# A two-layer hybrid backbone on one core: where the conditioning products are issued, and how their weights lie in memory

## The chip, the cores and the metric

One core of one Trainium2 chip. The metric is the device time of one execution in microseconds; before the change the median of three runs is 2308.41 us (2298.91 to 2311.32).

## What is computed

Two layers of a diffusion backbone on 512 latent and 256 context tokens (768 in all) with 1024 features, in fp32. Each layer mixes tokens in three groups of heads that share one input projection and one output projection: latent attention with 8 heads, a gated DeltaNet (GDN, a scan over chunks of 64 tokens), and a gated linear attention (GLA, in two directions). A gated feed-forward with a convolution over tokens follows. Every sub-layer is wrapped in norms and in scale, shift and gate, which come from two conditioning vectors, one for latents and one for context:

```python
mod_x = [m[:, None, :] for m in jnp.split(jax.nn.silu(c) @ w_ada[i] + b_ada[i], N_MOD, axis=-1)]
mod_c = jnp.split(jax.nn.silu(c_ctx) @ w_ada[i] + b_ada[i], N_MOD, axis=-1)
hx = modulate(rmsnorm(x, norm_mix_pre[i]), mod_x[0], mod_x[1])
y_c, y_x = token_mixing(...)
x = x + mod_x[2] * rmsnorm(y_x, norm_mix_post[i])
hx = modulate(rmsnorm(x, norm_ffn_pre[i]), mod_x[3], mod_x[4])
x = x + mod_x[5] * rmsnorm(conv_ffn(hx, ...))
```

`w_ada` is 1024 x 6144 for each layer, 24 MB. Its six products are needed at different times: 0 and 1 ahead of the input projection, 2 behind the output projection, 3 and 4 ahead of the feed-forward, 5 behind it.

## The kernel before, in words

An fp32 product is made of three passes over operands split in two float32r parts. `wsplit` (L197) loads 512 KB of weights into a tile `wr` of a ring of three (`raw`, L194), and ScalarE (`wh`, L191) and VectorE (`wl`, L192) split it; `fprod` (L217) issues the products into the large PSUM banks `bb`. Small products take the banks a, b, c and d; `ab` (L183) gives them out in turn, among those that the phase names.

A layer runs as follows (`layer`, L311). `project_in` (L555) makes 20 blocks of the input projection; the GDN's preparation and scan are chains of small products, and `pace` feeds steps of the large products between them. `mla_project` makes keys, queries and values and stores them in DRAM (`Kd`, `Qd`). Then comes `attention` for pair 0 of the heads, `gla`, and `attention` for pairs 1 to 3. `pair` (L1303) loads the keys and queries of a pair into tiles of the ring `wr`, three or four loads for each pair. Then follow the products of `w_out`, a norm, and the feed-forward with 40 blocks of `ffn_w_in` and the products back. Pair 0 draws small banks from a and d, pairs 1 to 3 from a and b; GLA's own products take c and d.

GLA makes the products inside its chunks by halving: seven levels for the context and seven for the latents, each on VectorE (L1180 to L1183), ScalarE, GpSimd, VectorE and GpSimd (L1193), TensorE (banks c and d) and VectorE again (the predicated copies of L1202). Then it makes two and four output tiles (L1229).

The framework orders the instructions of each engine ahead of time, by priorities and a simulated timeline; each engine then executes its own list in order. Tiles of a ring are given out in program order: a load waits until the third tile before it has been read.

The conditioning products are a generator, `ada` (L466). An item of it is one of six modulations and a quarter of 1024 columns: two loads of 512 KB of `w_ada` (L478) into ring tiles, eight products with the vectors as stationary operand (16 records `a<-wr,cTs` in the trace, in one of the banks), a copy by ScalarE (`part`, L485), two products that add up the parts and transpose them (four records `a<-cst,part`), and a copy by VectorE into `modT` (L488). `tick(n)` (L458) runs n items of the generators in `self.bg`. Eight items of layer 0 (modulations 0 and 1) lead the program, with tiles of their own (`aw`). The other 16 of layer 0 (`later`) are put in `self.bg` in `project_in`, behind the first blocks of the GDN, and each further block ticks one. The 24 of layer 1 are put there at the start of layer 0's feed-forward, whose blocks tick one each:

```python
        if LM == 2:
            self.bg += later          # in project_in
...
        if not last:
            self.bg.append(self.ada(l + 1, range(6)))   # ahead of the feed-forward
```

Of the kernel before, what the change touches and what calls it, by code (L numbers as in the profile page):

```python
# [17 lines left out]
PSUM = bass.MemoryType.PSUM  # L18
# [3 lines left out]
T = 768  # L22
# [10 lines left out]
# columns of the feature-major parameter array  # L33
# [16 lines left out]
LM = 2  # L50
# [8 lines left out]
NF = 3                  # tiles of the GDN preparation under way at a time  # L59
# columns of the constant array  # L60
# [50 lines left out]
def rope_tables():  # L111
    """cos and signed sin on the rope rows, ones on the others: even heads, odd heads"""
# [23 lines left out]
class Net:  # L136
# [46 lines left out]
    def ab(self, tags=None):  # L183
        """a bank of PSUM, out of those of the phase or of the chain of work named"""
        tags = tags or self.tags
        self.turn[tags] = n = self.turn.get(tags, -1) + 1
        t = tags[n % len(tags)]
        return self.ps.tile([128, 512], F32, name=self.nm(t), tag=t, bufs=1)
# [8 lines left out]
    def wsplit(self, src, n=1024):  # L197
        """loads [128, n] weights and splits them in two float32r parts, 512 columns a piece"""
# [18 lines left out]
    def fprod(self, ps, wh, wl, xh, xl, segs, nk, order=None, off=256):  # L217
        """ps[:, 256 + token] = sum over k of w[:, k]^T x[k], in three float32r passes"""
# [13 lines left out]
    def pace(self, n):  # L232
        """some steps of the products that fill the tensor engine beside chains of small ones"""
# [7 lines left out]
    def rsqrt(self, out, ss, scale, bias):  # L241
        """out = 1 / sqrt(scale * ss + bias), small tiles"""
# [18 lines left out]
    def main(self):  # L261
# [20 lines left out]
        # the first two modulations lead; the norm needs all of x, then them  # L282
# [28 lines left out]
    def layer(self, l, later):  # L311
# [9 lines left out]
        # token mixing  # L321
# [11 lines left out]
        self.project_in(later)  # L333
# [10 lines left out]
        # pairs that need nothing of what the scan holds up run beside its end  # L344
# [17 lines left out]
        self.attention(A2, range(EP[l], 4), mh, ml, mixed)  # L362
        self.xt = []
# [9 lines left out]
        # output projection, norm, residual  # L373
# [17 lines left out]
        # feed-forward  # L391
        self.ph = 2
        self.tags = "abcd"
        if not last:
            self.bg.append(self.ada(l + 1, range(6)))
# [6 lines left out]
        def tail(s):  # L402
            """norm, residual, and the next layer's first norm for a segment"""
# [33 lines left out]
    def coefs(self, s, r):  # L437
        """modulation of sub-layer s for latent (0) or context (1) tokens: scale [128, 8], shift [128, 8]"""
# [8 lines left out]
    def gate(self, s):  # L447
        """gate times post-norm gain of sub-layer s: [128, 8] for latent and context tokens"""
# [17 lines left out]
    def ada(self, l, mods, raw=None):  # L466
        """products of the conditioning vectors with w_ada, a load at a time"""
# [3 lines left out]
        for m in mods:  # L471
            for h in range(4):
                c0 = m * 1024 + h * 256
                raws = []
                for k in range(2):
                    rt = (raw or self.raw)()
                    src = self.a["w_ada"][l, k * 512:(k + 1) * 512, c0:c0 + 256].rearrange("(k p) c -> p k c", p=128)
                    nc.sync.dma_start(rt.rearrange("p (k c) -> p k c", k=4), src)  # L478
# [13 lines left out]
    def rms(self, N, src, a, b, copy=False):  # L492
        """1 / rms over the features of tokens a..b, on all partitions (in PSUM)"""
# [32 lines left out]
    def post(self, N, s, seg, y, g=None):  # L526
        """x += gate * norm(y)"""
# [8 lines left out]
    def prenorm(self, N, s, seg, rb=None):  # L536
        """norm and modulation of x, in two float32r parts"""
# [17 lines left out]
    def project_in(self, later):  # L555
# [12 lines left out]
        def gate(x):  # L568
            """silu times the head norm's gain, kept in DRAM"""
# [10 lines left out]
        def misc():  # L580
            # rope key, GLA low rank, GDN gates
# [12 lines left out]
            # GLA's gates by direction: softplus of the negated, kept in DRAM  # L594
# [16 lines left out]
        # GDN: k, v, q; token-major, sums of squares of k and q  # L611
        Gp, self.G = self.pool("G", "right")
        self.ktok, self.vtok, qtok = tok(self.F, "ktok"), tok(self.F, "vtok"), tok(self.G, "qtok")
        ss = self.small(48, "kss")              # [k | q, t, h]
# [24 lines left out]
        def projections():  # L639
            # GLA: k, q, v token-major, kept in DRAM  # L640
# [50 lines left out]
        if LM == 0:  # L691
            self.bg += later
# [857 lines left out]
```

## Time and profile before

| | before |
|---|---|
| runs, us | 2298.91, 2308.41, 2311.32 (median 2308.41) |
| profiled execution: first to last instruction, us | 2300.4 |
| mean granted clock of TensorE | 0.935 |
| TensorE matmul busy, us | 2073.8 (90%) |
| VectorE busy, us | 1308.2 (57%) |
| ScalarE busy, us | 1008.7 (44%) |
| GpSimd busy, us | 536.1 (23%) |
| DMA, MB | 235.64 |
| 512 KB loads of w_ada into the ring | 80 |

The profiled execution's time is its span, 8 us under the median of the three runs and close to the fastest. PE is TensorE's matmuls, PEld its weight loads, DVE VectorE, ACT ScalarE, POOL GpSimd, SP the engine that issues DMAs. Busy shares are means over stages with different limits, so the rows further down are from single stages. In layer 0 of this execution the conditioning items of `project_in` lie between 100 and 375 us, the GDN scan between 266 and 478, GLA with attention beside it from 482 to 655, the products of `w_out` from there, and the feed-forward's conditioning items between 763 and 988.

### The profile page before, as it was taken

Reading aid. Unit: us, or ns where it says so; the run is one execution under the profiler, and the core shown is the slowest. Engines: PE = TensorE matmul, PEld = TensorE weight load, DVE = VectorE, ACT = ScalarE, POOL = GpSimd, SP = SyncE. Lnnn points to the kernel's source line nnn. Section 1 sums busy time; section 2 is a strip of 40 time slices with the busy share of each in tenths; the row PEclk is TensorE's granted clock in tenths of the full one; section 3 lists DMA queues with packets and bytes.
Section 4 is the critical chain, followed back from the end, with each engine's and each line's share of the span. In section 5 each row is a group of like instructions: output and inputs, shape, how many; then the busy total and the mean of one; then the engine's idle time right before and its main releaser. Section 6 shows DMA issues by size and latency. Waiting matters only on the chain. (4 is left out here: it accounts for less than half of the span.)

```text
span 2300.4 us, 44608 instructions
## 1 busy us (share of the span) xinstructions
PE 2073.8 (90%) x18168; PEld 1695.2 (74%) x18168; DVE 1308.2 (57%) x2474; ACT 1008.7 (44%) x1927; POOL 536.1 (23%) x897
## 2 busy tenths in 40 slices
PE   6898999988988799999999889899978887999996
PEld 3676877766667578888888677777766666888886
DVE  3454435678736743445454774555657647655566
ACT  4653323566454533323232456434446346543333
POOL 1442122245402310101010334322123503211102
PEclk9899999999899899999999987999988888999997
DMA  7233344421042454421222332122402043332322
GB/s 259 73 111 104 102 152 151 148 79 58 8 158 92 142 169 165 163 85 56 65 66 72 111 98 76 42 73 93 149 26 95 6 166 95 111 98 95 101 92 92
DMA packets 121998, 235.64 MB, mean 102 GB/s; under 512 B 9088, under 2 KB 74048, under 8 KB 121792
## 3 DMA queue, kind: packets, MB, share of 16 engines
q1 hardware_dynamic: 121792, 232.78, 30.9%
q8 instruction: 143, 2.34, 0.4%
q14 instruction: 63, 0.52, 0.1%
HBM read 204.04 MB, written 28.70 MB: 101 GB/s over the span
## 5 line engine op out<-in xcount | busy, mean ns | idle before, releaser
L212 PE MATMUL bb<-hh,wl 128*128 128x512 f32 (+1 forms) x1520 | 549.3, 362 | 17.6 <-DVE wl L192 8.0
L212 PE MATMUL bb<-hl,wh 128*128 128x512 f32 (+1 forms) x1520 | 545.0, 359 | 7.3 <-POOL hl L552 5.5
L192 DVE TENSOR_TENSOR wl<-wr,wh 128x512 fp32r<-128x512 f32 (+2 forms) x452 | 336.2, 747 | 364.8 <-ACT wh L191 363.7
L212 PE MATMUL bb<-hh,wh 128*128 128x512 f32 (+1 forms) x1520 | 541.2, 356 | 0.0
L191 ACT CAST wh<-wr 128x512 fp32r<-128x512 f32 (+2 forms) x452 | 274.4, 612 | 527.4 <-PE bb L212 359.2
L212 PEld LDWEIGHTS bb<-hh,wl 128*128 128x128 f32 x1520 | 294.2, 194 | 74.2 <-issue 11.1
L212 PEld LDWEIGHTS bb<-hl,wh 128*128 128x128 f32 x1520 | 294.2, 194 | 53.0 <-POOL hl L552 9.8
L212 PEld LDWEIGHTS bb<-hh,wh 128*128 128x128 f32 x1520 | 294.4, 194 | 39.9 <-issue 2.4
L212 PE MATMUL bb<-g,wh 128*128 128x512 f32 (+1 forms) x1024 | 264.0, 349 | 2.3 <-DVE g L192 2.3
L1426 POOL TENSOR_SCALAR y<-u,fmt 128x512 f32<-128x512 f32 (+2 forms) x88 | 81.3, 925 | 524.1 <-ACT u L811 522.6
L212 PEld LDWEIGHTS bb<-g,wh 128*128 128x128 f32 x1024 | 181.9, 195 | 27.6 <-DVE g L192 3.3
L212 PE MATMUL bb<-g,wl 128*128 128x512 f32 (+1 forms) x512 | 180.6, 354 | 21.5 <-DVE wl L192 8.5
L212 PEld LDWEIGHTS bb<-g,wl 128*128 128x128 f32 x512 | 99.4, 195 | 36.9 <-ACT g L191 9.3
L212 PE MATMUL bb<-mh,wl 128*128 128x256 f32 (+1 forms) x256 | 84.8, 332 | 22.5 <-DVE wl L192 15.4
L811 ACT ACTIVATE u<-bb,fmt 128x512 f32<-128x512 f32 (+1 forms) x118 | 69.1, 614 | 81.1 <-PE bb L212 81.0
L1453 DVE TENSOR_TENSOR y<-y,bb 128x512 f32<-128x512 f32 (+2 forms) x80 | 54.7, 685 | 82.9 <-PE bb L212 82.8
L507 POOL TENSOR_TENSOR acc<-acc,sq 128x256 f32<-128x256 f32 (+1 forms) x48 | 49.4, 1031 | 185.2 <-ACT sq L505 184.5
L1427 DVE SCALAR_TENSOR_TENSOR y<-u,fmt,y 128x512 f32<-128x512 f32 (+2 forms) x88 | 72.3, 822 | 28.9 <-POOL y L1426 28.9
L1365 ACT ACTIVATE P<-bb,ast,srq 128x768 f32<-128x768 f32 (+1 forms) x80 | 72.5, 907 | 30.5 <-DVE ast L1363 20.2
L212 PE MATMUL bb<-ml,wh 128*128 128x256 f32 (+1 forms) x256 | 83.5, 326 | 0.5
L212 PE MATMUL bb<-mh,wh 128*128 128x256 f32 (+1 forms) x256 | 82.2, 321 | 0.0
L1362 DVE TENSOR_REDUCE ast<-bb 128x1 f32<-128x768 f32 (+1 forms) x80 | 67.3, 844 | 25.3 <-PE bb L212 25.0
(509 smaller groups left out, 3720.1 us busy)
## 6 DMA issues: line engine op xcount, KB each, us to landing
wr<-in_ffn_w_in SPq DMA_DIRECT2D x92, 512.0 KB, 3.5
wr<-in_w_ada SPq DMA_DIRECT2D x80, 512.0 KB, 4.4
wr<-in_ffn_w_out SPq DMA_DIRECT2D x48, 512.0 KB, 3.5
wr<-in_w_in SPq DMA_DIRECT2D x40, 512.0 KB, 4.0
wr<-in_w_out SPq DMA_DIRECT2D x32, 512.0 KB, 3.5
aw<-in_w_ada SPq DMA_DIRECT2D x16, 512.0 KB, 8.9
x<-in_xT SPq DMA_DIRECT2D x16, 384.0 KB, 8.5
wr<-in_w_uq SPq DMA_DIRECT2D x16, 192.0 KB, 2.6
```

Source lines behind the costliest of these rows:

```text
L191: self.nc.scalar.copy(hi, src)
L192: (eng or self.nc.vector).tensor_tensor(lo, src, hi.bitcast(F32), op=ALU.subtract)
L212: self.nc.tensor.matmul(out, l, r, start=start, stop=stop)
L507: (nc.vector, nc.gpsimd)[k % 2].tensor_tensor(acc[k % 2], acc[k % 2], sq, op=ALU.add)
L811: nc.scalar.activation(u[:, a + o:b + o], ps[:, off + a:off + b], AF.Identity, bias=bias)
L1362: nc.vector.reduce_max(st[:, 0:1], sc, axis=AX)
L1365: nc.scalar.activation(P[:, :w], sc, AF.Exp, bias=st[:, 0:1], scale=self.srq[:, t:t + 1], accum_out=st[:, 1:2])
L1426: nc.gpsimd.tensor_scalar(yv, u[:, lo + 1:lo + 1 + n], cw[1], self.fm(P_FCB + i), op0=ALU.mult, op1=ALU.add)
L1427: nc.vector.scalar_tensor_tensor(yv, u[:, lo:lo + n], cw[0], yv, op0=ALU.mult, op1=ALU.add)
L1453: nc.vector.tensor_tensor(y, y, p, op=ALU.add)
```

## The change

Items move. The 16 items `later` of layer 0 and the 24 of layer 1 are put in `self.bg` ahead of attention of pair 0 in layer 0. Attention ticks one item for each query tile (six for each pair), GLA one for each level and one for each output tile; what is left after attention is drained. `project_in` and layer 0's feed-forward have none to tick any more. On the host `w_ada` is packed anew, so that a load of 512 KB has rows of 4 KB on 128 partitions instead of 1 KB rows, four for each partition; the products read the same bytes. Comments are dropped, and lines move by up to four.

```diff
@@ layer
-        self.project_in(later)
+        self.project_in()
...
         A2p, A2 = self.pool("A2")
+        self.bg += later
+        if not last:
+            self.bg.append(self.ada(l + 1, range(6)))
         with self.ahead(HA):
             self.attention(A2, range(EP[l]))
...
         self.attention(A2, range(EP[l], 4), mh, ml, mixed)
+        self.tick(99)
...
         self.tags = "abcd"
-        if not last:
-            self.bg.append(self.ada(l + 1, range(6)))
         Up, U = self.pool("U", "right")
@@ ada
-                c0 = m * 1024 + h * 256
...
-                    src = self.a["w_ada"][l, k * 512:(k + 1) * 512, c0:c0 + 256].rearrange("(k p) c -> p k c", p=128)
-                    nc.sync.dma_start(rt.rearrange("p (k c) -> p k c", k=4), src)
+                    nc.sync.dma_start(rt, self.a["w_ada"][l, 4 * m + h, k])
@@ project_in
-        if LM == 0:
-            self.bg += later
         drain(gdn(0))
-        if LM == 2:
-            self.bg += later
@@ gla, at the end of a level and of an output tile
+                self.tick(1)
...
+                self.tick(1)
@@ attention, at the end of a query tile
+                self.tick(1)
@@ pack
-    out["w_ada"] = f["w_ada"]
+    out["w_ada"] = f["w_ada"].reshape(L, 2, 4, 128, 24, 256).transpose(0, 4, 1, 3, 2, 5).reshape(L, 24, 2, 128, 1024)
```

The order of each engine's instructions moves with it, at two places above all. The first is SyncE's queue of loads, behind the weights of the values (`in_w_uv`). Before, it holds the loads of pair 1's keys and queries, then pair 2's, ahead of GLA's (`gv`, `h`):

```order
L200 DMA wr_5078<-in_w_uv 128x1024
L1314 DMA wr_6362<-Kd_688_4766 128x768
...
L1314 DMA wr_6368<-krope_437 128x768
...
L1314 DMA wr_6378<-Qd_713_4872 128x768
...
L1314 DMA wr_6384<-Qd_738_4990 128x768
L1314 DMA wr_6763<-Kd_694_4789 128x768
...
L1078 DMA gv_5517<-gvd_2272 128x1536
L1092 DMA h_5523<-gkd_2270 128x256
```

Now the loads of 25 conditioning items come first, of which the first and the last stand here; pair 1's follow them, the last one behind GLA's last store (`md`):

```order
L199 DMA wr_4790<-in_w_uv 128x1024
L478 DMA wr_4929<-in_w_ada 128x1024
...
L478 DMA wr_4931<-in_w_ada 128x1024
...
L478 DMA wr_6469<-in_w_ada 128x1024
...
L478 DMA wr_6471<-in_w_ada 128x1024
L1312 DMA wr_6525<-Kd_624_4478 128x768
L1312 DMA wr_6531<-krope_437 128x768
L1312 DMA wr_6541<-Qd_649_4584 128x768
L1046 DMA md_112_436<-zt_6380 256x1x256
L1312 DMA wr_6547<-Qd_674_4702 128x768
```

All of these loads but GLA's use the ring `wr`. Pair 1's four loads moved from right behind `in_w_uv` to behind the 50 loads of the 25 items.

The second is TensorE's order inside GLA. Before, products of a context level (`c<-q,x`, `d<-q,x`) stand between query-key products of pair 1 (`bb<-K,Q`), its transposes (`a<-cst,P`) and its products with the values (`b<-PT,V`):

```order
L212 MATMUL bb_6671<-K_1039_6364,Q10l_6381 128x256
L212 MATMUL bb_6671<-K_1040_6365,Q10h_6380 128x256
L212 MATMUL bb_6671<-K_1039_6364,Q10h_6380 128x256
L212 MATMUL c_5632<-q_901_5629,x_5622 64x128 x4
L212 MATMUL d_5638<-q_901_5629,x_5622 64x128 x4
L212 MATMUL b_6513<-PT_6502,V_5131 64x128
...
L215 MATMUL a_6547<-cst,P_6541 128x128 x4
...
L212 MATMUL c_5654<-q_905_5651,x_5644 64x128 x4
L212 MATMUL d_5660<-q_905_5651,x_5644 64x128 x4
```

Now only conditioning items (`a<-wr,cTs`, `a<-cst,part`) stand between the levels' products:

```order
L211 MATMUL a_5628<-wr_5624,cTs 32x256 x4
L211 MATMUL d_5588<-wr_5584,cTs 32x256 x4
L211 MATMUL d_5588<-wr_5586,cTs 32x256 x4
L211 MATMUL c_5612<-q_893_5609,x_5602 64x128 x4
L211 MATMUL a_5628<-wr_5626,cTs 32x256 x4
L211 MATMUL d_5588<-cst,part_5597 128x2 x2
L211 MATMUL c_5652<-q_901_5649,x_5642 64x128 x4
L211 MATMUL d_5618<-q_893_5609,x_5602 64x128 x4
L211 MATMUL a_5628<-cst,part_5637 128x2 x2
L211 MATMUL c_5684<-q_858_5437,x_5682 64x128 x4
L211 MATMUL d_5658<-q_901_5649,x_5642 64x128 x4
```

The products of pair 1 moved out of GLA. They begin behind its last item and its last output transposes (`d<-cst,s`):

```order
L211 MATMUL a_6366<-cst,part_6375 128x2 x2
L214 MATMUL d_6411<-cst,s_6401 128x128 x2
...
L211 MATMUL d_6420<-wr_6416,cTs 32x256 x4
L211 MATMUL d_6420<-wr_6418,cTs 32x256 x4
L211 MATMUL d_6420<-cst,part_6429 128x2 x2
L211 MATMUL a_6473<-wr_6471,cTs 32x256 x4
L214 MATMUL d_6463<-cst,s_6453 128x128 x2
L211 MATMUL a_6473<-cst,part_6482 128x2 x2
L211 MATMUL bb_6554<-K_1076_6527,Q10l_6544 128x512
L211 MATMUL bb_6554<-K_1076_6527,Q10l_6544 128x256
```

The first product of pair 2 likewise stands behind the last item that pair 1 ticks, and pair 3's behind pair 2's last.

## Rows read from the trace of the kernel before

**Rows 1.** the page, part 1: busy us (share of the span) xinstructions, by engine

```profile
PE 2073.8 (90%) x18168; PEld 1695.2 (74%) x18168; DVE 1308.2 (57%) x2474; ACT 1008.7 (44%) x1927; POOL 536.1 (23%) x897
```

**Rows 2.** windows of the conditioning products alone (tile cTs): length, busy us (xrecords), PEclk, DMA

```profile
762.50:825.00 62.50, 10.87 (x128) 2.92 (x128) 0.00 (x0) 0.86 0.59 187
825.00:987.50 162.50, 17.95 (x256) 6.69 (x256) 0.00 (x0) 1.00 0.47 158
```

**Rows 3.** windows of all engines, early feed-forward of layer 0: length, busy us, PEclk, DMA, GB/s

```profile
core 0: us, PE busy (x) PEld busy (x) DVE busy (x) ACT busy (x) POOL busy (x), PEclk, DMA share, GB/s
762.50:825.00 62.50, 48.45 (x333) 35.98 (x332) 38.06 (x75) 31.05 (x64) 17.61 (x37) 0.86 0.59 187
```

**Rows 4.** windows of all engines beside attention and GLA of layer 0

```profile
500.00:520.00 20.00, 16.46 (x245) 12.43 (x244) 18.96 (x49) 12.55 (x31) 15.91 (x25) 1.00 0.13 41
520.00:540.00 20.00, 14.61 (x127) 10.55 (x127) 19.73 (x51) 10.16 (x23) 12.64 (x11) 0.83 0.38 119
...
580.00:600.00 20.00, 16.66 (x95) 11.84 (x95) 15.29 (x30) 6.70 (x14) 12.99 (x17) 0.52 0.00 1
```

**Rows 5.** timeline of PE from 110 us: start, us, engine, line, op, out<-in

```profile
110.72 1.07 PE L212 MATMUL a<-wr,cTs 128*32 128x256 f32 x16
...
112.06 0.40 PE L212 MATMUL bb<-hl,wh 128*128 128x512 f32 x1
112.29 0.39 PE L212 MATMUL bb<-hh,wh 128*128 128x512 f32 x1
...
116.84 0.50 PE L212 MATMUL a<-cst,part 128*128 128x2 f32 x4
...
117.52 0.40 PE L212 MATMUL bb<-hh,wh 128*128 128x512 f32 x1
```

**Rows 6.** windows of all engines: loads at the start, a stretch of 4 KB rows

```profile
3.00:44.00 41.00, 28.93 (x184) 17.18 (x184) 7.84 (x20) 16.03 (x34) 6.10 (x6) 1.00 1.04 357
...
1860.00:1870.00 10.00, 9.26 (x44) 8.07 (x45) 6.12 (x10) 6.30 (x12) 0.00 (x0) 0.61 1.00 370
```

**Rows 7.** the page, part 6: DMA issues, count, KB each, median us to landing

```profile
wr<-in_ffn_w_in SPq DMA_DIRECT2D x92, 512.0 KB, 3.5
wr<-in_w_ada SPq DMA_DIRECT2D x80, 512.0 KB, 4.4
```

**Rows 8.** timeline of POOL: GLA's first instruction in layer 0

```profile
482.57 0.15 POOL L1079 MEMSET St<- 128x64 f32 x1 [6.48 <-DMA md<-zt]
```

**Rows 9.** waits of PE from 760 to 990 us: total, times, longest

```profile
PE bb L212 <- DVE wl L192: 4.6, 2, 4.1
PE b L212 <- DMA wr<-in_w_ada: 3.3, 2, 2.4
PE d L212 <- DMA wr<-in_w_ada: 2.6, 2, 1.8
PE c L212 <- DMA wr<-in_w_ada: 1.5, 1, 1.5
```

**Rows 10.** timeline of PE: the first product of w_out in layer 0

```profile
655.53 0.79 PE L212 MATMUL bb<-mh,wl 128*128 128x512 f32 x1 [0.31 <-ACT mh L191]
```

**Rows 11.** line L1104, GLA's scans of layer 0: min/median/max ns, first and last start

```profile
L1104 DVE TENSOR_TENSOR_SCAN h<-h,h x4: 665/948/1576, 489.8 to 530.2; 128x256 f32<-128x256 f32 x2, 128x512 f32<-128x512 f32 x2
```

**Rows 12.** line L1202, latent levels of GLA in layer 1

```profile
L1202 DVE COPY_PREDICATED A<-cst,c x5: 729/740/742, 1817.3 to 1833.5; 128x512 f32<-128x512 uint32 x5
```

**Rows 13.** line L1229, output tiles of GLA in layer 1

```profile
L1229 DVE TENSOR_TENSOR s<-s,c x4: 420/421/422, 1838.0 to 1850.8; 128x256 f32<-128x256 f32 x4
```

**Rows 14.** DVE by lines from 478 to 660 us, GLA's: busy, mean ns, idle before

```profile
L1145 DVE SCALAR_TENSOR_TENSOR St<-St,glgl,h 128x64 f32<-128x64 f32 x22 | 10.6, 483 | 0.6 <-ACT h L1139 0.2
...
L1068 DVE TENSOR_TENSOR zt<-c,zt 128x128 f32<-128x128 f32 x2 | 0.5, 284 | 0.0
```

**Rows 15.** line L1390, ends of query tiles in attention of layer 1

```profile
L1390 DVE TENSOR_TENSOR mo<-b,rd x2: 271/282/292, 1737.1 to 1753.8; 128x128 f32<-128x128 f32 x2
L1390 DVE TENSOR_TENSOR mo<-a,rd x2: 291/292/292, 1747.5 to 1760.3; 128x128 f32<-128x128 f32 x2
```

More of the change, by code (lines that the diff above doesn't have):

```diff
@@ L49 @@
 XT = (2, 0, 1, 0, 1, 0, 1, 0)
-LM = 2
 MOB = 1
@@ L552, in prenorm, with project_in @@
                 nc.gpsimd.tensor_tensor(lo, v, hi.bitcast(F32), op=ALU.subtract)
-    def project_in(self, later):
+    def project_in(self):
         nc, l, last = self.nc, self.l, self.last
```

## The prediction

> **What bounds the kernel now.** I read the page first: TensorE is busy nine tenths of the span [rows 1], the other engines at most 57%. So the first question about any added or removed product is whether TensorE has a gap for it at that place. I therefore read the windows view of three stretches. In the conditioning part of layer 0's feed-forward TensorE is full from 825 us on (the tile view shows that 256 of the 384 product records lie there), and between 762.5 and 825 us it is idle for 62.5 - 48.45 = 14 us [rows 2, 3]. Beside attention and GLA it is not full: of the windows between 500 and 600 us that are shown, it is busy 16.46, 14.61 and 16.66 us of 20, and in the last of these at a granted clock of 0.52 [rows 4]. The reader is to see two things in that group: these are the gaps that the change wants to fill, and VectorE is busy 18.96 and 19.73 us of 20 in the first two, so it is VectorE, not TensorE, that holds the stage there.
>
> **The frame of the sum.** The change takes no conditioning product away: 40 items (16 of layer 0, 24 of layer 1) move. Where TensorE is full, an item costs its own time, and taking it away gives that back. Where TensorE is idle it costs nothing. So the result is the idle time that the items fill, less the idle time that the new order makes.
>
> **Price of an item.** On a full TensorE the sixteen records of an item start at 110.72 and the second ordinary product behind them at 112.06; ordinary products follow each other by 0.23 us (112.06 to 112.29). That is 1.34 - 0.23 = 1.11 us. The four records behind ScalarE's copy take from 116.84 to 117.52, less one ordinary product: 0.45 us [rows 5]. Sum 1.56; I take 1.6 us.
>
> **Part one, the 4 KB rows.** The sixteen loads at the start (8.4 MB) run with the loads of x at 357 GB/s between 3 and 44 us, a stretch of 4 KB rows at 370 [rows 6]. 8.4 MB take 23.5 us at the one and 22.7 at the other: **-1 us**, between 0 and -2. The 80 later loads land 4.4 us after issue, loads of the same 512 KB in 4 KB rows after 3.5 [rows 7]; that matters only where somebody waits for them, below. The Trainium skill (DMA: Bandwidth & Descriptors, Specifications) gives 512 bytes as the smallest transfer at line rate, by which 1 KB rows lose nothing and this part is worth 0; the sum would be 1 us higher.
>
> **Part two, project_in loses 16 items.** 16 x 1.6 = 25.6 us. Attention of pair 0 runs beside the end of the GDN scan and now carries six items; in the new TensorE order four of them stand ahead of the scan's last products: +6.4. So GLA, which waits for the scan, starts **19 us earlier**, at about 463 instead of 482.57 [rows 8]. Bounds: -25.6 if the six find gaps, -8 if a third of the 16 lay in gaps already and the six cost in full.
>
> **Part three, the feed-forward loses 24 items.** 24 x 1.6 = 38.4, and with them TensorE's waits for their loads, 3.3 + 2.6 + 1.5 = 7.4 us: together 45.8. Next to be late there are split weights; TensorE already waits 4.6 us for one [rows 9]. I give back some 4 us to them: **-42 us**. Lower end: the 8 items in the stretch with 14 us idle (128 of the 384 records) were free, and the next wait replaces theirs: 16 x 1.6 = -25.6. Upper end -45.8.
>
> **Part four, attention and GLA take 34 items, and their order changes.** This is the large term. Every load of w_ada takes one of the three tiles of the ring `wr`, and so do the loads of K and Q of pairs 1 to 3; tiles are given out in program order. Before, pair 1's loads stand on SyncE's queue right behind the values' weights, and pairs 1 to 3 are computed in GLA's gaps. Now 50 loads of w_ada (25 items) stand ahead of pair 1's, and in TensorE's order pair 1 begins only behind GLA's last item; pairs 2 and 3 wait likewise for the items of the pair ahead. GLA and the three pairs, side by side before, run one after the other.
>
> Before: from GLA's start, 482.57, to the first product of w_out, 655.53 [rows 8, 10]: **173 us**.
>
> After, GLA alone with its 19 items: setup 17 us (7.2 from its start to the first scan at 489.8 [rows 11], then some 10 of VectorE work before the first level); seven latent levels at 4.05 (layer 1, without much attention beside them, five copies from 1817.3 to 1833.5 [rows 12]): 29; seven context levels of half the width: 19, bounded by half and by the whole of a latent level (14 and 29); four latent output tiles at 4.27 (four from 1838.0 to 1850.8 [rows 13]): 17; the two context tiles and the latents' setup, half hidden: 10; items in bank d, which GLA's next product needs too: 6. Together **98 us**. The lower bound is VectorE's own work, 77 us in 17 rows of which the first and the last are shown [rows 14], and a tail: 86. Upper bound: second rival.
>
> Then pairs 1 to 3 alone. A latent query tile takes 6.4 us in layer 1 (ends at 1747.5, 1753.8, 1760.3 [rows 15]), with an item 8.0; a context tile, a third of the keys, 2.5, with an item 4.1. At a pair's end nothing else is there to run: the next pair's loads wait for the ring, land 3.5 us after issue [rows 7], are split, and the last small tile's chain drains. No row shows that gap; between 3.5 and 3.5 + 6.4 (a whole tile's time), I take 8, as everything in it is serial. Pairs 1 and 2: 4 x 8.0 + 2 x 4.1 + 8 = 48 each; pair 3 with the last three items: 4 x 6.4 + 2 x 2.5 + 3 x 1.6 + 4 = 39; the gap between GLA and pair 1: 6. Together **141 us**, between 118 (gaps of 3.5, half of the items hidden) and 165 (items also hold bank b against the transposes).
>
> 98 + 141 = 239 against 173: **+66 us**.
>
> **Sum.** -1 - 19 + 66 - 42 = **+4 us** on the profiled span of 2300.4: 2304. That execution lies 8 us under the median of the runs shown (2308.41, from 2298.91 to 2311.32), so on the median 2312 us. What a measurement of this kernel can tell from no change is about 0.5%, 11.5 us: I forecast no change that can be told.
>
> **Rivals.**
> *Faster: the items sink into the gaps, and GLA runs at VectorE's own pace.* For it: VectorE is saturated from 500 to 540 because attention's maxima and copies stand in GLA's way [rows 4]; alone, GLA has it to itself, with TensorE filled by items. Then GLA takes 86, and the pairs 118 + 1: 205 against 173 is +32 instead of +66, hence 2312 - 34 = **2278**. Against it: a level is a chain over four engines, and pairs end with nothing to cover them.
>
> *Slower: the ring is too short for GLA.* An item's second load can only be issued when the first tile of the item before it has been read; it lands 3.5 us later and the item takes 1.6. TensorE executes in order, and in its new order GLA's level products stand behind items. If an item comes every 5.1 us, this decides as soon as it exceeds the level's 4.05 [rows 12]: 19 x 5.1 + 17 + a tail of 13 = 127 instead of 98, and part of the same in the pairs: +30 to +38, **2346**. Against it: the ring has three tiles, so that one load is always ahead, and two loads of 512 KB need only 2.8 us at 370 GB/s.
>
> *The clock.* In the window from 580 to 600 us TensorE runs at the lower level for nearly the whole of it; (1 - 0.52) x 16.66 = 8 us of work are lost there, and 14.61 x 0.17 = 2.5 from 520 to 540 [rows 4]. Items in these gaps may keep the clock up: 2312 - 10.5 = **2301**. But the new gaps between the pairs cost the same coin. The Trainium skill (TensorE: Matmul & The Clock Gate, What's actually happening) says that the throttled state is the default and activity releases it; rows 4 agree in so far as the low clock follows gaps.
>
> *The items were largely free in the feed-forward*, so that the change does not free what it says: part three at its lower end, 2312 + 16 = **2328**. Against: 16 of 24 items lie where TensorE has no gap at all [rows 2].
>
> **How the numbers follow.** Chances: forecast 0.34, faster rival 0.26, slower rival 0.24, clock 0.10, free items 0.06. The forecast's own uncertainty (GLA -12, pairs -23/+24, scan start -7/+11) puts a tenth of it under 2297 and a fifth over 2320, the clock case half under 2297. Faster by over 0.5%: 0.26 + 0.05 + 0.03 = 0.34; within 0.5%: 0.24 + 0.05 = 0.29; slower: 0.24 + 0.06 + 0.07 = 0.37. Both signs hold much: the likeliest case alone spans 2295 to 2330; the range that holds it 8 times in 10 takes in both large rivals, 2266 to 2352.
>
> **What would show it.** In the changed profile: GLA's first memset near 463; its last head norm near 561; pair 1's first product after that; gaps of 6 to 9 us on TensorE at the three pair ends; w_out's first product near 702; feed-forward windows without conditioning records and the whole of it some 42 us shorter; head loads ending about 1 us earlier. The forecast is wrong if pairs 1 to 3 still run inside GLA, if GLA takes over 115 or under 88 us, or if the feed-forward is shortened by less than 30.

## The result, and the profile after

The changed kernel takes **2371.19 us** (median of four runs, 2364.88 to 2376.32), the kernel before 2309.84 (four runs on the same chip, 2298.91 to 2311.32): a ratio of **1.0277 [1.0247, 1.0308]**. That is 59 us above the predicted time and 19 us above the top of the range. The profiled execution has a span of 2363.1 us, against 2300.4 before: 62.7 us more, while no engine's busy time moves by more than 23 us. On the changed kernel's page, part 1 answers to [rows 1]:

```profile
PE 2096.4 (89%) x18168; PEld 1717.0 (73%) x18168; DVE 1330.5 (56%) x2474; ACT 1009.9 (43%) x1924; POOL 528.6 (22%) x897
```

TensorE has as many records as before and 22.6 us more busy time, and its mean granted clock is 0.913 against 0.935. 22.6 us of busy time do not make 62.7 us of span; idle time does. To find the place, I cut both spans at five marks: GLA's first memset in layer 0 [rows 8], its last head norm (tile `zt`), the first product of `w_out` [rows 10], the last product back from the feed-forward (tile `g`), and GLA's first memset in layer 1. The marks of the changed kernel, from the tile view (min/median/max ns, first and last start) and from the timeline of PE:

```profile
L1075 POOL MEMSET St<- x1: 151/151/151, 462.9 to 462.9; 128x64 f32 x1
L1064 DVE TENSOR_TENSOR zt<-d,zt x12: 273/281/292, 533.1 to 618.8; 128x128 f32<-128x128 f32 x12
L211 PE MATMUL bb<-g,wh x640: 276/392/582, 969.5 to 1415.1; 128*128 128x512 f32 x80, 128*128 128x256 f32 x80
```

```profile
761.10 0.51 PE L211 MATMUL bb<-mh,wl 128*128 128x512 f32 x1
```

The two of before that have no row further up:

```profile
L1068 DVE TENSOR_TENSOR zt<-d,zt x12: 271/280/292, 554.7 to 647.3; 128x128 f32<-128x128 f32 x12
L212 PE MATMUL bb<-g,wh x640: 276/388/581, 883.7 to 1346.3; 128*128 128x512 f32 x80, 128*128 128x256 f32 x80
```

Differences of these marks give the stretches of a span; the other kernels are those of the next section. Each line is one execution, and two kernels that do the same work in a column can differ there by up to 7 us (before and e1_layout in the fifth). "Stage" is the sum of the second and the third column, the time that the prediction put at 173 before and 239 after.

| kernel | start to GLA | GLA | GLA to w_out | w_out to last product back | to GLA of layer 1 | to the end | span |
|---|---|---|---|---|---|---|---|
| before | 482.6 | 164.7 | 8.2 | 690.8 | 389.1 | 565.0 | 2300.4 |
| after | 462.9 | 155.9 | 142.3 | 654.0 | 384.6 | 563.4 | 2363.1 |
| e1_layout | 484.2 | 163.9 | 8.4 | 691.6 | 382.2 | 564.6 | 2294.9 |
| e3_no_gla_items | 455.3 | 170.6 | 77.6 | 680.7 | 386.4 | 560.6 | 2331.2 |
| e4_serial | 463.4 | 145.8 | 138.8 | 677.8 | 384.3 | 565.8 | 2375.9 |
| e5_pairs_ahead | 462.7 | 165.8 | 53.8 | 676.0 | 383.7 | 563.6 | 2305.6 |
| e6_two_pairs_ahead | 455.9 | 166.3 | 119.4 | 655.5 | 379.1 | 561.4 | 2337.6 |
| e7_serial_filled | 462.4 | 160.7 | 143.8 | 675.2 | 389.6 | 562.4 | 2394.1 |
| e8_in_layer1 | 482.2 | 165.0 | 7.9 | 664.6 | 397.3 | 625.2 | 2342.2 |
| e9_gla_items_free | 460.3 | 199.2 | 35.2 | 684.8 | 387.5 | 567.7 | 2334.7 |
| e10_attention_layer1 | 481.4 | 164.0 | 8.6 | 667.5 | 405.0 | 579.2 | 2305.7 |

The reader is to see the second line against the first. 19.7 us are gained ahead of GLA, 36.8 between w_out and the last product back, 6.1 behind it; all of that and 62.7 more goes into the stage, 173 us before and **298** now. Pairs 1 to 3 no longer run in GLA's gaps but behind it: GLA itself is 9 us shorter, and 134 more follow it.

Beside GLA, TensorE has the items, and its granted clock is low. The windows of all engines, with the columns of [rows 3], which answer to [rows 4]:

```profile
480.00:500.00 20.00, 12.70 (x144) 6.83 (x136) 16.57 (x31) 5.08 (x14) 15.52 (x22) 0.50 0.40 136
500.00:520.00 20.00, 15.56 (x148) 8.99 (x148) 14.98 (x35) 5.03 (x11) 8.19 (x10) 0.66 0.49 157
520.00:540.00 20.00, 17.07 (x172) 10.65 (x168) 6.41 (x26) 6.81 (x15) 6.33 (x6) 0.74 0.50 173
540.00:560.00 20.00, 13.97 (x166) 9.52 (x168) 13.99 (x28) 5.81 (x10) 14.08 (x18) 0.52 0.44 141
560.00:580.00 20.00, 14.64 (x132) 10.05 (x130) 15.27 (x23) 3.91 (x5) 12.11 (x10) 0.50 0.26 83
```

No engine is full in any of them. VectorE, which was at 18.96 and 19.73 of 20 in [rows 4], is down to between 6 and 17, and GLA is hardly faster for it.

### The profile page after: what moved, and what is told of

Its sections match the earlier page's. It is cut to its first block, busy times and chain, and to the rows that moved or that the text cites. A ratio compares the mean times of both kernels' runs of the same rounds, so it can differ in the third digit from the quotient of the medians.

```text
span 2363.1 us, 44653 instructions
## 1 busy us (share of the span) xinstructions
PE 2096.4 (89%) x18168; PEld 1717.0 (73%) x18168; DVE 1330.5 (56%) x2474; ACT 1009.9 (43%) x1924; POOL 528.6 (22%) x897
## 3 DMA queue, kind: packets, MB, share of 16 engines
q8 instruction: 143, 2.34, 0.4%
## 5 line engine op out<-in xcount | busy, mean ns | idle before, releaser
L191 DVE TENSOR_TENSOR wl<-wr,wh 128x512 fp32r<-128x512 f32 (+2 forms) x452 | 347.9, 771 | 360.3 <-ACT wh L190 358.5
L211 PEld LDWEIGHTS bb<-g,wl 128*128 128x128 f32 x512 | 99.0, 194 | 35.8 <-ACT g L190 9.7
L1363 ACT ACTIVATE P<-bb,ast,srq 128x768 f32<-128x768 f32 (+1 forms) x80 | 72.5, 907 | 37.0 <-DVE ast L1361 14.6
L1366 POOL TENSOR_SCALAR dg<-cst,ast 128x128 f32<-128x128 f32 x80 | 32.6, 413 | 214.6 <-DVE ast L1361 78.7
```

Of the source, the lines that this page charges most:

```text
L191: (eng or self.nc.vector).tensor_tensor(lo, src, hi.bitcast(F32), op=ALU.subtract)
L211: self.nc.tensor.matmul(out, l, r, start=start, stop=stop)
L1363: nc.scalar.activation(P[:, :w], sc, AF.Exp, bias=st[:, 0:1], scale=self.srq[:, t:t + 1], accum_out=st[:, 1:2])
L1366: nc.gpsimd.tensor_scalar(dg, ident, st[:, 1:2], 1.0, op0=ALU.mult, op1=ALU.mult)
```

## The experiments

**Theory one:** GLA is a chain that needs some 150 us whatever runs beside it. Before, the three pairs were hidden in it; the change's time is the overlap that is gone. **Theory two**, the rival nearest to the prediction: GLA alone is short, as forecast (98 us), and the items stretch it, by their waits for loads, their time on TensorE or the banks they hold. Beside these stand two questions: what an item costs at each place, and whether some other place for the items gains what the feed-forward gives back.

**The rows alone** (e1_layout). The kernel before, with only the loads' layout of the change:

```diff
-                    src = self.a["w_ada"][l, k * 512:(k + 1) * 512, c0:c0 + 256].rearrange("(k p) c -> p k c", p=128)
-                    nc.sync.dma_start(rt.rearrange("p (k c) -> p k c", k=4), src)
+                    nc.sync.dma_start(rt, self.a["w_ada"][l, 4 * m + h, k])
```

> The kernel before with nothing changed but the 4 KB rows of w_ada. Both theories of the loss (that GLA and pairs 1 to 3 now run one after another, or that the items inside GLA hold it up) leave this part alone: -1 us at the start of the program, up to -5 if the loads' waits in project_in and the feed-forward shrink; 2304 to 2309 us, a ratio of 0.998 to 1.000.

Measured: 2302.28 us, ratio 0.9985 [0.9963, 1.0008]. The loads of `w_ada` land 4.1 us after issue, against 4.4 [rows 7]. The layout is worth nothing that can be told, and the rest of the change makes the whole difference.

**Items out of GLA, the rest as in the change** (e3_no_gla_items). Attention ticks its 24 items and the feed-forward the last 16:

```diff
@@ gla, at the end of a level and of an output tile
-                self.tick(1)
...
-                self.tick(1)
@@ layer, behind attention
-        self.tick(99)
```

> The changed kernel without the two ticks in GLA and without the drain behind attention: attention ticks 24 items, the feed-forward the other 16. In TensorE's order pair 1 then stands inside GLA again. Theory one (the loss is the lost overlap): the stage from GLA's start to w_out falls from 298 us to about 200, the feed-forward is some 35 us longer than in the changed kernel, total near 2308. Theory two (the 19 items inside GLA stretch it): GLA falls from 156 to about 100 us; pair 1 hides in it, pairs 2 and 3 behind it, stage near 200 as well. The total does not tell them apart, GLA's own length does: about 150 to 165 by the first, about 100 by the second.

Measured: 2325.34 us, ratio 1.0086 [1.0063, 1.011], 17 above the value expected. GLA takes 170.6 us, which speaks for theory one: it ticks no item and has the pairs only partly beside it, and it is no faster than before. It is no test of GLA alone, though, since nine of attention's items run in its time (144 of their records, 16 each). The stage, 248.2, is the miss. Each pair's loads now stand behind the items of the pair ahead in the ring, and part of the overlap stays lost.

**The order of the change without its items in GLA** (e4_serial). e3, and at each place where the change ticks an item in GLA two GpSimd copies of one column take a ring tile each. Nobody reads them; they only stand for the two loads in the ring's program order.

```diff
+                for _ in range(0 if last else 2):
+                    nc.gpsimd.tensor_copy(self.raw()[:, 0:1], A[:, 0:1])
```

> As the kernel without GLA items, but in place of GLA's ticks of layer 0 a copy of one column of GLA's tile A into two tiles of the ring wr each time, so that the loads of pairs 1 to 3 still wait for GLA: GLA alone, with neither items nor attention beside it. Theory one: GLA alone takes about 150 us even so, the stage 285 or more, the total (with 16 items back in the feed-forward) near 2390. Theory two: GLA alone takes about 98 us as I had forecast, the stage 240, the total near 2345.

Measured: 2377.29 us, ratio 1.0306 [1.0287, 1.0325]. This run decides about the order. GLA ticks no item, and the stage takes 284.6 us, 112 of the 125 that the change adds: the ring tiles taken ahead of the pairs are enough to lose the overlap. (Some 20 of the 112 at most can be the copies' own, below.) GLA itself takes 145.8 us. Its marks and its levels, from the tile views:

```profile
L1074 POOL MEMSET St<- x1: 152/152/152, 463.4 to 463.4; 128x64 f32 x1
L1197 DVE COPY_PREDICATED A<-cst,c x7: 429/433/446, 485.9 to 509.1; 128x256 f32<-128x256 uint32 x7
L1197 DVE COPY_PREDICATED A<-cst,c x7: 718/728/736, 535.0 to 568.9; 128x512 f32<-128x512 uint32 x7
L1197 DVE COPY_PREDICATED A<-cst,d x7: 714/722/734, 536.1 to 569.7; 128x512 f32<-128x512 uint32 x7
L1226 DVE TENSOR_TENSOR s<-s,c x6: 405/421/422, 515.0 to 601.5; 128x256 f32<-128x256 f32 x6
L1063 DVE TENSOR_TENSOR zt<-d,zt x12: 280/281/292, 519.5 to 609.2; 128x128 f32<-128x128 f32 x12
```

For GLA's own length the run says less. Up to the end of its last latent copy, 570.4, nothing of pairs 1 to 3 is beside it, and that takes 107.0 us. Behind it pair 1 already runs: the next work in ScalarE's order is the cast of pair 1's keys, which wait for their load, and GLA's first latent output tile stands behind it. Pair 1's first product comes 25 us ahead of GLA's last head norm:

```profile
573.63 3.27 ACT L190 CAST K<-wr 64x768 fp32r<-64x768 f32 x4 [11.27 <-DMA wr<-Kd]
576.81 0.36 ACT L1225 COPY s<-c 128x256 f32<-128x256 f32 x1
584.55 1.01 PE L211 MATMUL bb<-K,Q10l 128*128 128x512 f32 x2
```

So this end takes 38.8 us, where the changed kernel, without a pair beside it, needs 24.8. With that end GLA alone would be near 132, an estimate. The 28 copies in the levels are busy for 5.1 us in all, and GpSimd waits for the level ahead of them:

```profile
POOL wr L1200 <- DVE A L1197: 14.1, 8, 2.7
```

Part of that wait is hidden, since the next step often has to wait for ScalarE anyway. Taken off in full, these 19 us leave some 112. GLA alone thus lies between about 112 and 132 (a few us lower if the four items in the changed kernel's end cost something there): theory two's 98 is out, of which 92 were for GLA without its items, and so is the 150 of theory one. Its windows show no full engine; VectorE comes nearest.

```profile
483.00:503.00 20.00, 8.48 (x112) 5.82 (x112) 16.79 (x36) 3.84 (x10) 13.77 (x27) 0.50 0.18 54
523.00:543.00 20.00, 9.74 (x164) 8.11 (x164) 13.65 (x25) 5.61 (x9) 12.66 (x18) 0.51 0.08 27
```

**Is it the clock?** (e7_serial_filled) The granted clock is 0.50 in these windows, so e4 with TensorE kept busier: three products into bank b for each level and output tile, on the level's own data, which nobody reads (they are added to the computation):

```diff
+                for _ in range(0 if last else 3):
+                    self.mm(self.ab("b")[:, :256], self.c("ident"), xf[:, n:n + 256], True, True)
```

> The serial kernel without items in GLA, plus three idle products behind each level and output tile of GLA in layer 0 (into bank b, from that level's own tile, read by nobody), 60 in all. If GLA's 146 us alone are a matter of TensorE's half clock there (0.5 in most of its windows), the filled kernel's clock rises and GLA falls by 15 us or more, to 130 or less. If they are the chain over VectorE, ScalarE and GpSimd, GLA stays at 140 to 155 us whatever the clock does.

Measured: 2390.57 us, ratio 1.0374 [1.0348, 1.0401]. GLA takes 160.7 us, 15 more than in e4 and outside both expectations. The windows say that the test worked in the first half only:

```profile
523.00:543.00 20.00, 16.30 (x224) 10.82 (x224) 13.94 (x30) 6.10 (x12) 10.61 (x13) 0.85 0.09 28
543.00:563.00 20.00, 9.87 (x74) 6.77 (x70) 8.89 (x15) 2.11 (x2) 14.82 (x23) 0.50 0.00 0
```

From 523 to 543 the clock rose from 0.51 to 0.85, and VectorE did not do its work any sooner (13.94 us against 13.65). From 543 on it stayed at 0.50. The products stand in TensorE's order and delay the chain themselves, as ScalarE's wait for those in bank b shows, so the run can't say what the half clock is worth; it shows that these extra products do not shorten GLA.

```profile
ACT x L1182 <- PE b L211: 9.9, 2, 6.9
```

**The overlap back, by program order** (e5_pairs_ahead). e3, and in layer 0 each pair issues the next pair's loads ahead of its own items:

```diff
-            if p:
-                self.pair(A2, p)
+            for x in (p, p + 1) if not last and p < 3 else (p,):
+                if x not in self.qs:
+                    self.pair(A2, x)
```

> As the kernel without GLA items, but the loads of pair p+1 of layer 0 stand ahead of pair p's items in program order, so that no pair waits for the items of the pair before. Theory one: full overlap is back while 24 items sit in the gaps; stage 173 to 190 us, GLA start about 470, 16 items left in the feed-forward: total 2280 to 2300, faster than both. Theory two: the same, since no items stand in GLA; but GLA beside attention would then be about 100 us long and the stage under 170.

Measured: 2306.53 us, ratio 1.0003 [0.9989, 1.0017]. Against e3 the stage falls from 248.2 to 219.6 and the whole loss is gone, but the 2280 to 2300 expected was missed. Against before, the stage still has 46.7 us more, and 18 items more than pair 0's stand in it: 2.6 us for each, if all of it is put down to them. That is more than an item costs on a full TensorE in the feed-forward (below).

**Two pairs' loads ahead of GLA** (e6_two_pairs_ahead). The whole change, with the loads of pairs 1 and 2 ahead of GLA's items in program order:

```diff
+        if not last:
+            self.pair(A2, 1)
+            self.pair(A2, 2)
         with self.ahead(HG):
             self.gla()
```

> The changed kernel, all 40 items where it puts them, but the loads of pairs 1 and 2 stand ahead of GLA in program order, so that no item's load is ahead of them in the ring. If the ring alone makes the order, pairs 1 and 2 run inside GLA again, the stage falls from 298 to about 230 us and the total to about 2305. If the small PSUM banks hold them as well (GLA's items take banks a and d in turn, ahead of pair 1's transposes in bank a, and pair 1's own items are behind GLA's in the ring), only its first query-key products move, and the total stays within 15 us of the changed kernel's: 2355 to 2372.

Measured: 2342.57 us, ratio 1.0169 [1.0138, 1.02], between the two values expected. The stage fell only from 298.2 to 285.7. With its operands in place, pair 1 makes its first query-key products between 471 and 496 us, but its products with the values start at 631.0, behind GLA: the ring is no longer what holds it. What is left in program order ahead of the pairs are the small banks that the items take (a and d in GLA; pairs 1 to 3 draw from a and b), and the items that the pairs tick themselves.

**Those two taken away as well** (e9_gla_items_free). e6, with GLA's items in banks c and d, and no items in pairs 1 to 3; the 15 left over go to the feed-forward:

```diff
+                tags, self.tags = self.tags, "cd"
                 self.tick(1)
+                self.tags = tags
@@ attention
-                self.tick(1)
+                if p == 0:
+                    self.tick(1)
@@ layer, behind attention
-        self.tick(99)
```

> The changed kernel with GLA's 19 items kept, but so that nothing of attention is behind them: the loads of pairs 1 and 2 stand ahead of GLA, GLA's items take banks c and d, pairs 1 to 3 tick no items, and the 15 that are left go to the feed-forward. If the lost overlap is the cause of the 125 us, the pairs run inside GLA again with the items beside them: GLA 165 to 180 us, the stage 180 to 200 instead of 298, the stretch from w_out to layer 1's GLA about 1060, total 2275 to 2300, faster than both kernels. If items inside GLA cost much by themselves, GLA takes 190 us or more and the total stays at 2305 or above.

Measured: 2339.72 us, ratio 1.0137 [1.0114, 1.0159], where 2275 to 2300 was expected. The stage is 234.4, of which 35.2 are the tail: most of the overlap is back. But GLA itself, now with pairs and items beside it, takes 199.2 us:

```profile
L1066 DVE TENSOR_TENSOR zt<-d,zt x6: 272/281/293, 564.9 to 659.5; 128x128 f32<-128x128 f32 x6
```

That is 34.5 us more than before, for 19 items. The gaps of GLA and the pairs together are not free. How much of the 34.5 comes from the banks c and d, which the items now share with GLA's own products, was not tested.

**Layer 1's items behind layer 1's attention** (e8_in_layer1). e1, with 16 of layer 1's items in one piece behind its attention, ahead of its `w_out`, and eight left in the feed-forward:

```diff
+        if last:
+            self.bg.append(self.ada(l, (2, 3, 4, 5)))
+            self.tick(99)
...
-            self.bg.append(self.ada(l + 1, range(6)))
+            self.bg.append(self.ada(l + 1, (0, 1)))
```

> The kernel before with the 4 KB rows, where the 16 items of layer 1 that are needed late (modulations 2 to 5) leave layer 0's feed-forward and are drained behind layer 1's attention in program order, so that nothing waits for them: TensorE is idle there for some 20 us between 1800 and 1860 and for 15 between 1900 and 1960. If an item costs its own time only where TensorE is full, 16 x 1.9 = 30 us come back in the feed-forward and 5 to 12 are paid in layer 1: 2280 to 2290. If items cost as much there as in attention and GLA of layer 0 (46 us for 18 in the kernel with pairs ahead), nothing is won: 2305 or more.

Measured: 2341.86 us, ratio 1.0163 [1.0133, 1.0192], over 50 us above the first value expected (2280 to 2290) and within the second (2305 or more). The feed-forward gives back what it should (664.6 us from w_out to the last product back, 26.2 less than before), but `w_out` of layer 1 begins 62 us later after GLA's start. The records of the items alone, between 1850 and 1900 us:

```profile
1850.00:1900.00 50.00, 22.23 (x168) 4.77 (x168) 0.00 (x0) 0.50 0.86 301
```

168 records are 10.5 items of 16, so one comes every 4.8 us, with the core's DMA engines at 0.86 and TensorE's granted clock at 0.50. TensorE waits 13.6 us for loads of `w_ada` between 1840 and 1905 us:

```profile
PE b L212 <- DMA wr<-in_w_ada: 8.0, 7, 2.0
PE a L212 <- DMA wr<-in_w_ada: 5.6, 4, 4.3
```

Which of the loads and the clock sets the pace was not separated; 2 MB of other loads (`xres`) pass in the same 50 us.

**Layer 1's items in layer 1's attention** (e10_attention_layer1). The same 16 items ticked one by one by layer 1's query tiles, with the next pair's loads ahead as in e5:

```diff
+        if last:
+            self.bg.append(self.ada(l, (2, 3, 4, 5)))
...
+                if last:
+                    self.tick(1)
```

> The kernel before with the 4 KB rows, where layer 1's 16 late items are ticked by layer 1's own attention (one a query tile), the next pair's loads ahead of them. The drain behind attention took some 45 us for 16 items in the kernel with items in layer 1, since nothing hid them; here attention and GLA hide them in part. 13 to 18 us come back in layer 0's feed-forward; the stage of layer 1 (125 us before) gets 10 to 31 us longer: 2290 to 2315. Under 2290 only if TensorE's idle 20 us at GLA's end take most of them.

Measured: 2303.37 us, ratio 0.9977 [0.9959, 0.9995], inside the expected band. Its ratio is the lowest of all versions, but e1's interval holds it, so it can't be told from the layout alone. The feed-forward gave back 23.3 us (667.5 against 690.8), and layer 1 took 30 (405.0 + 579.2 against 389.1 + 565.0).

A ring of their own for the items was not tried.

## Why the prediction was wrong

**Part one, the 4 KB rows: the sign right, the size too small, and nothing of it in the total.** -1 us was forecast, between 0 and -2. The last products on a head tile `aw` start at 44.3 us before, at 42.6 in e1 and at 40.9 in the changed kernel, 1.7 and 3.4 us earlier; e1's total can't be told from before. The 357 GB/s of [rows 6] hid it, since that window runs on past the last load. Up to 40 us, before and after:

```profile
3.00:40.00 37.00, 25.50 (x152) 15.19 (x153) 7.51 (x18) 15.28 (x32) 6.10 (x6) 1.00 1.06 365
3.00:40.00 37.00, 27.90 (x184) 16.16 (x184) 7.74 (x20) 15.86 (x34) 6.10 (x6) 1.00 1.00 392
```

With the DMA engines busy throughout, the loads of the start run 7% faster with `w_ada` in rows of 4 KB (389 GB/s in e1), so that the reading by which 1 KB rows lose nothing does not hold here. The Trainium skill (DMA: Bandwidth & Descriptors, Specifications) gives some 358 GB/s as the limit of HBM for one core. The trace differs: 365 and 392 GB/s over these 37 us lie above it, and so does the 370 of [rows 6].

**Part two, GLA's start: right.** Forecast 19 us earlier, at about 463; measured 462.9.

**Part three, the feed-forward: right within its bounds.** 42 us were forecast, between 25.6 and 45.8. w_out to the last product back is 36.8 shorter, 1.53 for each of the 24 items, against the 1.6 taken from [rows 5] and the 1.75 with their waits. The runs with 16 items gone from it agree (26.2 in e8, 23.3 in e10: 1.64 and 1.46 each), so that the rival by which the items were largely free there falls.

**Part four: the order right, one term wrong by 58 us.** That pairs 1 to 3 would begin only behind GLA's last item is what happened: PE's timeline shows the first product of pair 1 behind it.

```profile
619.00 1.01 PE L211 MATMUL a<-cst,part 128*128 128x2 f32 x4 [1.59 <-ACT part L485]
623.03 1.01 PE L211 MATMUL bb<-K,Q10l 128*128 128x512 f32 x2 [3.02 <-DVE Q10l L191]
```

The pairs were forecast at 141 us, and 142.3 were measured, in part by luck: from first product to first product pair 1 took 55.0 us and pair 2 50.0, where 48 each were forecast, and the rest (the gap ahead of pair 1 and pair 3 up to `w_out`) 37.3 instead of 45. The idle time at a pair's end is smaller than the 8 us taken, 2.11 and 2.34 us around the last item of pair 1 and 1.99 and 2.07 around that of pair 2, and the tiles took longer by more than that:

```profile
675.04 0.61 PE L211 MATMUL b<-cst,part 128*128 128x2 f32 x4 [2.11 <-ACT part L485]
677.99 1.01 PE L211 MATMUL bb<-K,Q00l 128*128 128x512 f32 x2 [2.34 <-DVE Q00l L191]
...
724.99 0.91 PE L211 MATMUL b<-cst,part 128*128 128x2 f32 x4 [1.99 <-ACT part L485]
727.97 1.01 PE L211 MATMUL bb<-K,Q10l 128*128 128x512 f32 x2 [2.07 <-DVE Q10l L191]
```

The step that failed is "GLA alone with its 19 items: 98 us". It took **155.9**. Measured by its own pieces (e4 ticks no items; pair 1 is beside its last piece alone):

| piece | forecast | e4_serial | after |
|---|---|---|---|
| setup, to the first context copy | 17 | 22.5 | 26.6 |
| seven context levels | 19 | 23.5 | 25.8 |
| context's output tiles and the latents' setup, to the first latent copy | 10 | 25.6 | 36.5 |
| seven latent levels, to the end of the last copy | 29 | 35.4 | 42 |
| the rest: latent output tiles, head norms | 17 | 38.8 | 25 |
| items in bank d | 6 | - | - |
| sum | 98 | 145.8 | 155.9 |

The marks of the changed kernel are the predicated copies, of the context and of the latents:

```profile
L1198 DVE COPY_PREDICATED A<-cst,c x7: 428/432/450, 489.5 to 514.9; 128x256 f32<-128x256 uint32 x7
L1198 DVE COPY_PREDICATED A<-cst,c x7: 714/732/745, 551.8 to 585.2; 128x512 f32<-128x512 uint32 x7
L1198 DVE COPY_PREDICATED A<-cst,d x8: 444/723/734, 521.7 to 593.3; 128x512 f32<-128x512 uint32 x7, 128x256 f32<-128x256 uint32 x1
```

The first four pieces were forecast at 75 us; they take 107 in e4 and 131 in the changed kernel. So of the 58 us, 32 are there without any item (at the least 13, if e4's copies lengthen the chain by their whole 19), 24 come with the 15 items that GLA ticks in these pieces (at the most 43), and 8 lie in the last piece with the other four. For all 19 items 6 us were forecast. Both halves of the term were too small, the chain alone and what the items do to it; e4 gives their shares only within these bounds.

The "slower" rival came nearer to the time (2346), and its mechanism is there in part: it wanted 29 us more for GLA from waits for the items' loads, and between 460 and 622 us TensorE waits 14.6 us for them in 10 waits, 9.6 of these ahead of the first context copy. They stand beside a chain that waits for VectorE and GpSimd.

```profile
PE a L211 <- DMA wr<-in_w_ada: 14.6, 10, 4.5
PE c L211 <- POOL q L1189: 4.7, 3, 1.9
PE d L211 <- DVE A L1198: 3.0, 2, 2.6
```

Three readings of the trace of before led to it.

*The rate of a level was taken from the fastest rows.* [Rows 12] hold five of layer 1's seven latent copies, from 1817.3 on. Asked for all seven, the same line answers:

```profile
L1202 DVE COPY_PREDICATED A<-cst,c x7: 726/736/742, 1797.7 to 1833.5; 128x512 f32<-128x512 uint32 x7
```

So the first two took 19.6 us and the seven 35.8 from the first start to the last, and not 29. Attention was still beside them, so this row is no measure of GLA alone either; e4 needed 35.4, with its copies in it.

*The setup of the latents was put at "half hidden".* Nothing in the profile showed it hidden. In e4 25.6 us pass there between the context's last copy and the first latent one, together with the context's output.

*The sum was not held against a whole.* The kernel before has a shorter GLA in layer 1: latents only, no context levels, no context output. It runs from 1735.4 to 1854.1, 118.7 us:

```profile
L1079 POOL MEMSET St<- x1: 152/152/152, 1735.4 to 1735.4; 128x64 f32 x1
...
L1068 DVE TENSOR_TENSOR zt<-d,zt x8: 279/282/292, 1842.6 to 1854.1; 128x128 f32<-128x128 f32 x8
```

With the forecast's own 19 us for context levels on top, that is 138. Pairs run beside it there, so it is not a proof, but 98 for a GLA with more work in it should have been explained against that row. The reason that I gave, VectorE at 19.73 of 20 [rows 4], was read too far: attention filled gaps of the chain on VectorE, but did not make the chain as long as it is. Without attention VectorE has idle time (16.79 and 13.65 of 20 in e4), and GLA went from 164.7 to somewhere between 112 and 132, not to 92.

With 156 in place of 98 the sum is +62 on the span; the profile has +62.7. That they agree so closely is luck: the feed-forward gave 5 us less than forecast, and the rest of the program, forecast as unchanged, took 6 less.

**The clock rival** falls. It let the items keep the clock up; the windows of the changed kernel have 0.50 to 0.74 from 480 to 580 us, lower than [rows 4].

**The faster rival**, GLA at VectorE's own pace of 86 us, falls: GLA took 155.9 in the changed kernel, and some 112 at the least in the estimate from e4.

What stays open is why the chain needs 112 to 132 us alone: how much of it is TensorE's half clock in e4, and how much the hand-over between engines. e7 could not separate them. Nor does any run show how an item that takes 1.6 us on a full TensorE lengthens the chain by as much or more.

## What to carry to other kernels

When a change breaks an overlap, its price is the whole of the shorter branch, unless the longer one really gets faster when alone; take that length from a whole phase that was measured, the nearest there is, and not from the fastest rows of its pieces. Before moving work into a phase with idle engine time, look at what shares its rings and banks in program order: here the two ring tiles of each item put three unrelated pairs behind it, and that order alone cost most of what was lost (e4). A saturated engine beside a chain of small steps shows that the gaps are used, not how much shorter the chain would be without the neighbour.

## What the runs showed that I had not expected

- **Items were free in no place that was tried.** By the differences between kernels, one costs 1.5 us in the full feed-forward, 2.6 beside attention and GLA (e5: 46.7 us for 18), 1.8 in GLA with pairs beside it and the items in GLA's banks c and d (e9: 34.5 for 19), 1.6 or more in a GLA without pairs (24 us for 15, the changed kernel against e4), and 3.9 in one piece by themselves (e8: 62 us for 16). These are prices of a place with its order, not of an item alone. No version that moved them gained more than 0.3% on before.
- **Busy time at a low clock overstates work.** From 560 to 580 us the changed kernel's TensorE is busy 14.64 us of 20 at a granted clock of 0.50. The records of an item show what that means: in the stage's bank a, where most of them ran at the low level (1.2 GHz), the median record takes 632 ns; in bank b, in the pairs, 379:

```profile
L211 PE MATMUL a<-wr,cTs x160: 376/632/637, 468.8 to 616.2; 128*32 128x256 f32 x160
L211 PE MATMUL b<-wr,cTs x240: 379/379/403, 641.1 to 757.2; 128*32 128x256 f32 x120
```

So a window that looks 73% full held, by the granted clock, half of that in work at the upper level, or 0.6 of it by the two medians.
